# A planned encoder kernel: x is normalised before its split, projections are evacuated straight from PSUM, the pooling matrix goes into the input weights, and the list schedule gets other costs

## The chip, the cores and the metric

The kernel runs on one core of one Trainium2 chip. The metric is the device time of one launch in microseconds (us); lower is better. Engines are named PE (matmul; PEld is its weight load), DVE (vector), ACT (scalar), POOL (GpSimd) and SP (the queue that issues the DMAs here).

## The reference

An encoder of 2 layers with shared weights is applied to two sequences (x_prompt and x_sample) of 1024 tokens and 1024 channels each, and ends in an RMSNorm. One layer is, cut to what matters:

```python
hdn = rmsnorm(x, norm_g)                    # x * rsqrt(mean(x*x) + eps) * g
z = hdn @ w_in                              # 1024 x 3072, 12 blocks of 256 columns
a_v, a_g, b_q, b_k, b_v, b_g, c_u, c_g, d_q, d_k, d_v, d_g = split(z, 12)
y_a = pool_mixer(a_v, pool_w, pool_scale) * silu(a_g)      # (window mean - u) @ pool_w[group] * scale
y_b = dilated_attention(rope(b_q), rope(b_k), b_v) * silu(b_g)
y_c = s5_mixer(c_u, ...) * silu(c_g)                       # SSM over time, gelu, GLU
y_d = neighbourhood_attention(d_q, d_k, d_v, rpb) * silu(d_g)
x = x + concat(y_a, y_b, y_c, y_d) @ w_out
```

The window mean works along time and pool_w along channels, so the two can change places.

## The kernel before

**Layout and number format.** x is kept transposed, 128 channels on the partitions and time along the free dimension, as 8 blocks of 128 channels x 1024 tokens, handled in halves h of 512 tokens. Products with w_in and w_out are made in three terms: each operand is split into a rounded high part (`xh`, `whi`, `yh`) and the rest (`xl`, `wlo`, `yl`), and hi*hi, hi*lo and lo*hi are summed in PSUM (`terms`). One half of one 128-column block of w_in is so 8 x 3 = 24 matmuls of 512 columns.

**Iterations.** `run` goes over 4 iterations (s, l): sequence 0 layer 0, sequence 1 layer 0, sequence 0 layer 1, sequence 1 layer 1; they are numbered 0 to 3 here. Each iteration records the steps of `STEPS`: `na` (neighbourhood attention), `dil` (dilated attention), `ssm` and `sout` (the SSM), `pool`, then `x` (`load_x`: the next iteration's x), `out6723` (the half of the output product that needs y blocks 6, 7, 2 and 3), `out` (the other half). `setup0` and `setup1` make the SSM's tables for a layer.

**From x to a projection.** `load_x` fetches 16 pieces of 128 x 512; `split_x` makes the high part on ACT (scaled with the norm's g) and the rest on DVE. ACT squares each piece and POOL adds the squares. `stats` turns these sums into 1/rms per token (8 small matmuls, a Newton iteration on DVE) and spreads it over the partitions as a tile `rstd` (transposes and ACT copies). rstd isn't in xh and xl; it is multiplied in when a projection leaves PSUM. `project` loads and splits a block of w_in, accumulates a half in a bank of the group mm (3 banks) and calls an evacuation: `scaled` is the DVE product with rstd that writes an SBUF tile of the group z (6 tiles) and frees the bank. What follows works from that tile: `gate` (tanh on ACT, one more DVE product), `split_q` and `split_k` (ACT copies, DVE differences), `rotated` (ACT copies that swap partitions, products with sin and cos on POOL, a DVE sum, then split_q or split_k). `values` makes v with tokens on the partitions and takes rstd as a per-partition scalar.

**Pooling.** `pooling` projects u, sums windows on DVE, takes the difference to u, splits the result and pool_w, multiplies them in three terms (2 halves x 3 matmuls), and DVE multiplies by the scale and the gate.

**The order of the work.** Nothing runs when its line is reached. A `Recorder` takes down every operation with its dependencies; `order` then is a list scheduler that gives each engine a fixed order. It plays time forward: an operation takes `cost` nanoseconds, its results are usable after a latency by pair of engines (`LAT`), and a free engine takes the ready operation with the smallest `prio = idx + cls + base`. `cls` is LATE (+10^6) for the matmuls of `product`, so that projections fill the time in which no other matmul is ready, SOON (-10^6) for evacuations and weight loads. `room` gives a tile out only when all threads can still end. `emit` writes the operations in that order; on the chip each engine takes its instructions in that fixed order and waits at semaphores. `record` treats every access to a PSUM tile as one to the whole bank, and orders two accesses only if one of them writes.

All instructions are issued in one helper, so the profile gives every one the same line, L461; tiles tell them apart. The profile's names follow a buffer's first tile: vz and kt stand for the mm banks (and others), ss and rb for the t banks, ss and rstd for the two tiles that hold rstd, zq, zs, zk, kt and wto for tiles of the group z.

## Time and profile before

| | |
|---|---|
| time, median of 3 runs | 2167.78 us (2164.34 to 2167.82) |
| the profiled execution, its own time | 2156.2 us |
| its span, first to last instruction | 2154.4 us |
| mean granted TensorE clock | 0.975 of full speed |
| instructions | 33356 |

The profile is of one execution. Busy time of an engine is the time in which at least one of its instructions was in work; an idle time has a releaser, what the waiting instruction waited for last. "xN" counts instructions.

### The profile page before, as it was taken

How to read it: one execution, taken by the hardware profiler on the slowest of the kernel's cores; microseconds unless marked ns; L12 is line 12 of the kernel's file. 1: busy time of each engine (PE TensorE's matmuls, PEld its weight loads, DVE VectorE, ACT ScalarE, POOL GpSimd, SP SyncE). 2: the span in 40 equal slices, each digit the busy share in tenths (PEclk: the TensorE clock that was granted, in tenths of full speed). 3: DMA queues.
4: the chain of work that ended last, by engine and by line, in shares of the span. 5: the costliest groups of instructions: out<-in, count | busy, mean ns of one | idle time of the engine just before them, and what ended most of it. 6: DMA issues, size and time to landing. Idle time of an engine off the chain costs nothing.

```text
span 2154.4 us, 33356 instructions
## 1 busy us (share of the span) xinstructions
PE 1984.5 (92%) x10980; PEld 1656.8 (77%) x10980; DVE 1572.2 (73%) x3400; ACT 1095.0 (51%) x2486; POOL 573.6 (27%) x464
## 2 busy tenths in 40 slices
PE   7989999889999999889998999888899999998997
PEld 7757778667888888767787788767678878786777
DVE  7998688987246578788688667888734666888835
ACT  4438595134156688225125678823433766861315
POOL 3218231336200202124017142234543001202103
PEclk8999999999999999999999999999999999999999
DMA  4456535638855444646886543454588645346375
GB/s 160 147 167 188 169 95 169 191 106 269 270 168 160 134 145 118 202 134 217 265 250 187 175 151 105 129 180 155 197 283 278 214 144 173 106 139 201 115 243 178
DMA packets 321853, 381.12 MB, mean 177 GB/s; under 512 B 50832, under 2 KB 196752, under 8 KB 321680
## 3 DMA queue, kind: packets, MB, share of 16 engines
q1 hardware_dynamic: 321680, 378.99, 56.4%
q8 instruction: 87, 1.43, 0.3%
q14 instruction: 86, 0.70, 0.1%
HBM read 268.88 MB, written 112.10 MB: 177 GB/s over the span
## 4 chain that ended last, share of the span: by engine, by line
PE 44%; DVE 22%; DMA 14%; ACT 8%; issue 7%; POOL 3%; SPq 3%; DVEq 0%; POOLq 0%; ACTq 0%
PE vz L461 30%; DMA nv<-vd 4%; PE kt L461 4%; PE no L461 4%; DVE X L461 3%; DMA p<-x 3%; PE ss L461 3%; SPq L461 3%; PE rb L461 2%; DVE p L461 2%; DVE zq L461 1%; DVE gate L461 1%; DVE arena L461 1%; DVE H L461 1%; ACT p L461 1%
## 5 line engine op out<-in xcount | busy, mean ns | idle before, releaser
L461 PE MATMUL vz<-xh,whi 128*128 128x512 f32 x1324 | 531.7, 402 | 3.7 <-DVE zq L461 1.8
L461 PE MATMUL vz<-xl,whi 128*128 128x512 f32 x1324 | 531.5, 401 | 1.5 <-DVE xl L461 1.5
L461 PE MATMUL vz<-xh,wlo 128*128 128x512 f32 x1324 | 530.8, 401 | 0.8 <-POOL wlo L461 0.8
L461 POOL TENSOR_TENSOR wlo<-raw,whi 128x512 fp32r<-128x512 f32 x128 | 179.8, 1406 | 590.7 <-ACT whi L461 437.8
L461 ACT ACTIVATE whi<-raw 128x512 fp32r<-128x512 f32 x248 | 155.6, 627 | 340.5 <-DMA raw<-in_w_in 120.8
L461 PEld LDWEIGHTS vz<-xh,whi 128*128 128x128 f32 x1324 | 251.7, 190 | 49.9 <-issue 2.9
L461 PEld LDWEIGHTS vz<-xh,wlo 128*128 128x128 f32 x1324 | 251.8, 190 | 44.6 <-issue 2.1
L461 PEld LDWEIGHTS vz<-xl,whi 128*128 128x128 f32 x1324 | 252.2, 191 | 43.7 <-DVE xl L461 2.0
L461 PE MATMUL vz<-whi,xh 128*128 128x256 f32 x464 | 135.2, 292 | 15.1 <-ACT xh L461 8.6
L461 ACT ACTIVATE p<-p,st 128x256 f32<-128x256 f32 x256 | 128.3, 503 | 30.6 <-DVE st L461 29.3
L461 DVE TENSOR_TENSOR p<-vz,p 128x512 f32<-128x512 f32 x86 | 58.4, 687 | 112.8 <-DMA p<-x 96.8
L461 PE MATMUL vz<-whi,xl 128*128 128x256 f32 x464 | 134.2, 289 | 0.1
L461 PE MATMUL vz<-wlo,xh 128*128 128x256 f32 x464 | 133.8, 289 | 0.1
L461 PE MATMUL vz<-yh,whi 128*128 128x512 f32 x300 | 121.5, 405 | 9.6 <-DVE p L461 5.2
L461 PE MATMUL vz<-yl,whi 128*128 128x512 f32 x300 | 120.0, 400 | 0.0
L461 PE MATMUL vz<-yh,wlo 128*128 128x512 f32 x300 | 119.5, 400 | 0.0
L461 PEld LDWEIGHTS vz<-whi,xh 128*128 128x128 f32 x464 | 91.3, 197 | 16.9 <-ACT xh L461 8.6
L461 ACT ACTIVATE p<-p,nmx 128x384 f32<-128x384 f32 x128 | 78.2, 612 | 43.1 <-DVE nmx L461 42.1
L461 DVE TENSOR_TENSOR D<-ss,D 128x128 fp32r<-128x128 f32 (+2 forms) x195 | 85.5, 461 | 9.8 <-ACT D L461 8.2
L461 PEld LDWEIGHTS vz<-whi,xl 128*128 128x128 f32 x464 | 91.3, 197 | 1.0 <-issue 0.4
L461 PEld LDWEIGHTS vz<-wlo,xh 128*128 128x128 f32 x464 | 91.2, 197 | 0.8 <-issue 0.4
L461 PE MATMUL no<-D,bv 128*128 128x256 f32 x512 | 88.7, 293 | 3.1 <-DVE D L461 1.5
(489 smaller groups left out, 4616.1 us busy)
## 6 DMA issues: line engine op xcount, KB each, us to landing
raw<-in_w_in SPq DMA_DIRECT2D x192, 256.0 KB
low<-wlo SPq DMA_DIRECT2D x128, 256.0 KB
wlo<-low SPq DMA_DIRECT2D x120, 256.0 KB
x<-p SPq DMA_DIRECT2D x112, 256.0 KB
p<-x SPq DMA_DIRECT2D x88, 256.0 KB
nbias<-in_na_bias SPq DMA_DIRECT2D x48, 384.0 KB
nv<-vd SPq DMA_DIRECT2D x256, 64.0 KB
raw<-in_w_out SPq DMA_DIRECT2D x128, 128.0 KB
```

The costliest lines, as they stand in the source:

```text
L461: getattr(engines[op.eng], op.method)(*[real(a) for a in op.args], **{k: real(v) for k, v in op.kw.items()})
```

## The change

Five things are changed together.

1. `load_x` multiplies a piece by g and rstd on DVE (in place) before it is split, in the iterations 1 to 3. rstd must be known then: the sums of squares are taken where the output product writes the new x (`layer_out`, ACT squares, POOL adds), and for the second sequence's first layer in a new step `sq` (`sum_squares`), of the lowest priority, in iteration 0. `stats` is cut in two: `stats` gives r by token, `spread` makes the rstd tile. Iteration 0 keeps the old way (`self.rstd` isn't None).
2. Evacuations read PSUM: `scaled` returns the bank itself when there is no rstd, and ACT copies or applies tanh, and DVE multiplies, out of the bank. The product with cos moves from POOL to DVE. Evacuations and the split of y run as SOON.
3. pool_w is multiplied into the a_v columns of w_in on the chip (`pool_weights`, steps `poolw0` and `poolw1`, plain fp32 matmuls, result kept in DRAM); the product in `pooling` goes.
4. `cost` has new constants.
5. Factors 0.5 and 0.125 move to other operations.

```diff
-            if op.method == "transpose":
-                return 107 * n / 128
+            if m == "transpose":
+                return 108 * n / 128
             f32r = op.reads[0].dtype == F32R
-            return n / 2.4 + 1 if f32r and n >= 256 else max(n, 128) / 0.6 + 1
+            half = 0.7 if out.dims[0][1] == 64 else 1
+            return n / 2.4 + 13 if f32r and n >= 256 else half * (max(n, 128) / 0.6 + 9)
         if op.eng == "DVE":
-            m = op.method
+
+            wide = sum(v.tile.space == "SB" and v.dims[1:] != [[1, 1]] for v in op.reads) > 1
+            port = 150 if wide and n >= 256 else 0
             if m == "reciprocal":
-                return 68 + 6.5 * n / 0.96
+                return 145 + 6.1 * n
+            if m == "tensor_tensor_scan":
+                return 350 + 2.1 * n
             if not ps and m in ("tensor_copy", "tensor_scalar", "tensor_scalar_mul", "memset"):
-                return 66 + n * 0.525
-            return 68 + n * 1.042 + (8 if m == "tensor_tensor_reduce" else 0) + (61 if isinstance(op.kw.get("scalar"), View) else 0)
+                return 145 + n * 0.53
+            return 145 + n * 1.055 + port + (85 if m == "tensor_tensor_reduce" else 0) + (60 if isinstance(op.kw.get("scalar"), View) else 0)
         if op.eng == "ACT":
-            return (52 if ps else 93) + n * 0.833 + (93 if "accum_out" in op.kw else 0) + (94 if len(op.reads) > 1 else 0)
+            return (180 if ps else 205) + n * 0.833 + (187 if "accum_out" in op.kw else 0) + (88 if len(op.reads) > 1 else 0)
         if op.eng == "POOL":
-            if op.method == "memset":
-                return 40 + n * 0.5
+            if m == "memset":
+                return 90 + n * 0.84
             spread = any(s == 0 and c > 1 for v in op.reads for s, c in v.dims[1:])
-            return 148 + n * (1.67 if spread else 2.1)
+            return 190 + n * (1.8 if spread else 2.4)
...
-        src = self.T[name][l, mt]
+        src = self.T[name][l, mt] if (name, l, mt) not in self.made else self.made[name, l, mt]
...
+    def sum_squares(self, src):
 
         nc = self.nc
         ss = nc.tile([128, S], F32, "rs", "ss")
+        lead = [self.mains[-1]] * 2
+        for h in range(2):
+            sl = slice(512 * h, 512 * h + 512)
+            for k in range(8):
+                sq = self.z("xsq")
+                nc.sync.dma_start(out=sq, in_=src[k, h], after=lead[-2])
+                if k == 0:
+                    lead.append(nc.scalar.activation(ss[:, sl], sq, AF.Square))
+                else:
+                    nc.scalar.activation(sq, sq, AF.Square)
+                    lead.append(nc.gpsimd.tensor_tensor(out=ss[:, sl], in0=ss[:, sl], in1=sq, op=ALU.add))
+        return self.stats([[ss[:, :512]], [ss[:, 512:]]])
+
+    def load_x(self, src, l, r):
+
+        nc = self.nc
+        rstd = self.spread(r)
+        self.rstd = self.rcol = None
         lead = [self.mains[-1]] * 3
         for h in range(2):
             sl = slice(512 * h, 512 * h + 512)
             for k in range(8):
                 raw = self.z("xraw")
                 nc.sync.dma_start(out=raw, in_=src[k, h], after=lead[-3])
-                lead.append(self.split_x(k, sl, raw, l)[0])
-                self.add_square(ss[:, sl], raw, k == 0)
-        self.rstd = self.stats([[ss[:, :512]], [ss[:, 512:]]])
-        self.rcol = self.cols
+                nc.vector.scalar_tensor_tensor(out=raw, in0=raw, scalar=self.norm_g[:, l, k : k + 1], in1=rstd[:, sl], op0=ALU.mult, op1=ALU.mult)
+                lead.append(nc.scalar.activation(self.xh[k][:, sl], raw, AF.Copy))
+                nc.vector.tensor_tensor(out=self.xl[k][:, sl], in0=raw, in1=f32(self.xh[k])[:, sl], op=ALU.subtract)
...
-    def scaled(self, dst, ps, sl, scale=None, shape=lambda a: a):
-
-        nc = self.nc
-        nc.cls = SOON
-        a, b = shape(ps), shape(self.rstd[:, sl])
-        if scale is None:
-            nc.vector.tensor_tensor(out=dst, in0=a, in1=b, op=ALU.mult)
-        else:
-            nc.vector.scalar_tensor_tensor(out=dst, in0=a, scalar=scale, in1=b, op0=ALU.mult, op1=ALU.mult)
-        nc.cls = 0
-
-    def evac_to(self, dst, scale=None):
-        return lambda ps, sl, h: self.scaled(dst(h), ps, sl, scale)
-
-    def gate(self, l, mt, f=0.5):
+    def scaled(self, ps, sl):
+
+        if self.rstd is None:
+            return ps
+        z = self.z("zq")
+        self.nc.vector.tensor_tensor(out=z, in0=ps, in1=self.rstd[:, sl], op=ALU.mult)
+        return z
+
+    def evac_to(self, dst, shape=lambda a: a):
+        def ev(ps, sl, h):
+            self.nc.cls = SOON
+            self.nc.scalar.activation(dst(h), shape(self.scaled(ps, sl)), AF.Copy)
+            self.nc.cls = 0
+        return ev
+
+    def gate(self, l, mt):
 
         nc = self.nc
         g = self.slot([128, S], "gate")
 
         def ev(ps, sl, h):
-            z, th = self.z("zg"), self.z("th")
-            self.scaled(z, ps, sl, f)
-            nc.scalar.activation(th, z, AF.Tanh, scale=0.5 / f)
+            nc.cls = SOON
+            z, th = self.scaled(ps, sl), self.z("th")
+            nc.scalar.activation(th, z, AF.Tanh, scale=0.5)
             nc.vector.scalar_tensor_tensor(out=g[:, sl], in0=th, scalar=1.0, in1=z, op0=ALU.add, op1=ALU.mult)
+            nc.cls = 0
...
-                r = self.rcol[n]
-                nc.scalar.activation(vt[:, i, :, 0], ps, AF.Copy, scale=r)
-                nc.vector.scalar_tensor_tensor(out=vt[:, i, :, 1], in0=ps, scalar=r, in1=f32(vt)[:, i, :, 0], op0=ALU.mult, op1=ALU.subtract)
+                if self.rcol is None:
+                    nc.scalar.activation(vt[:, i, :, 0], ps, AF.Copy)
+                    nc.vector.tensor_tensor(out=vt[:, i, :, 1], in0=ps, in1=f32(vt)[:, i, :, 0], op=ALU.subtract)
...
+            op = self.nc.scalar.activation(at(K[h][d]), z[d], AF.Copy, scale=scale)
+            self.nc.scalar.activation(at(K[h][e]), z[d], AF.Copy, scale=scale)
+            if scale == 1.0:
+                self.nc.vector.tensor_tensor(out=at(kl[h][d]), in0=z[d], in1=at(f32(K[h])[d]), op=ALU.subtract)
+            else:
+                self.nc.vector.scalar_tensor_tensor(out=at(kl[h][d]), in0=z[d], scalar=scale, in1=at(f32(K[h])[d]), op0=ALU.mult, op1=ALU.subtract)
...
-                z = self.z("zq")
-                self.scaled(z.rearrange("p (w r c) -> p r w c", w=4, r=8), ps, sl, None, lambda a: a.rearrange("p (r w c) -> p r w c", r=8, w=4))
-                self.split_q(Q, z.rearrange("p (w x) -> p w x", w=4), lambda t: t.rearrange("p (w g x) -> p g w x", w=4, g=2)[:, h])
+                nc.cls = SOON
+                z = self.scaled(ps, sl).rearrange("p (r w c) -> p w r c", r=8, w=4)
+                self.split_q(Q, z, lambda t: t.rearrange("p (w g r c) -> p g w r c", w=4, g=2, r=8)[:, h])
+                nc.cls = 0
 
             def fk(ps, sl, h):
-                z = self.z("zk")
-                self.scaled(z, ps, sl, 0.125)
-                self.split_k(K, kl, z, lambda t: t[:, sl], h == 0)
+                nc.cls = SOON
+                self.split_k(K, kl, self.scaled(ps, sl), lambda t: t[:, sl], h == 0, 0.125)
...
+            y = self.scaled(ps, sl).rearrange("p (j c) -> p c j", c=4)
             z, zs = self.z("zr"), self.z("zs")
-            self.scaled(by4(z), ps, sl, scale, lambda a: a.rearrange("p (j c) -> p c j", c=4))
             for i in range(4):
                 d, e = 32 * i, 32 * (i ^ 1)
-                nc.scalar.activation(zs[d : d + 32], z[e : e + 32], AF.Copy)
+                nc.scalar.activation(by4(zs)[d : d + 32], y[e : e + 32], AF.Copy, scale=scale)
+            if scale == 1.0:
+                nc.vector.tensor_tensor(out=by4(z), in0=y, in1=by4(cos[:, sl]), op=ALU.mult)
+            else:
+                nc.vector.scalar_tensor_tensor(out=by4(z), in0=y, scalar=scale, in1=by4(cos[:, sl]), op0=ALU.mult, op1=ALU.mult)
+            nc.cls = 0
             nc.gpsimd.tensor_tensor(out=zs, in0=zs, in1=sin[:, sl], op=ALU.mult)
-            nc.gpsimd.tensor_tensor(out=z, in0=z, in1=cos[:, sl], op=ALU.mult)
...
+    def pool_weights(self, l):
+
+        nc = self.nc
+        for m in range(2):
+            made = self.own([128, 8, 128], "wav", F32, "DRAM")
+            wt, pw = self.slot([128, S], "wavt"), self.z("pool_w")[:, :128]
+            nc.sync.dma_start(out=wt, in_=self.T["w_av"][l, m])
+            nc.sync.dma_start(out=pw, in_=self.T["pool_w"][:, l, m])
+            for i in range(2):
+                ps, t = self.bank("t", "wav"), self.z("wav")
+                for k in range(4):
+                    nc.tensor.matmul(ps[:, 128 * k : 128 * k + 128], wt[:, 512 * i + 128 * k : 512 * i + 128 * k + 128], pw, start=True, stop=True)
+                nc.scalar.activation(t, ps, AF.Copy)
+                nc.sync.dma_start(out=made[:, 4 * i : 4 * i + 4], in_=t.rearrange("p (k x) -> p k x", k=4))
+            self.made["w_in", l, MT_AV + m] = made
...
-            pw = self.z("pool_w")[:, :128]
-            nc.sync.dma_start(out=pw, in_=self.T["pool_w"][:, l, m], after=self.mains[-1])
-            if POOLR:
-                pr = self.slot([128, 2, 128], "pwr", F32R)
-                nc.scalar.activation(pr[:, 0], pw, AF.Copy)
-                nc.gpsimd.tensor_tensor(out=pr[:, 1], in0=pw, in1=f32(pr)[:, 0], op=ALU.subtract)
-                wh, wl = self.halves_of(w, "pw")
-            for h in range(2):
-                ps = self.bank("mm", "pool")
-                sl = slice(512 * h, 512 * h + 512)
-                if POOLR:
-                    self.terms(ps, [pr[:, 0]], [pr[:, 1]], [wh[:, sl]], [wl[:, sl]])
-                else:
-                    nc.tensor.matmul(ps, pw, w[:, sl], start=True, stop=True)
-                nc.vector.scalar_tensor_tensor(out=gt[:, sl], in0=ps, scalar=self.pool_s[:, l, m : m + 1], in1=gt[:, sl], op0=ALU.mult, op1=ALU.mult)
+            nc.vector.scalar_tensor_tensor(out=gt, in0=w, scalar=self.pool_s[:, l, m : m + 1], in1=gt, op0=ALU.mult, op1=ALU.mult)
...
-            def f(ps, sl, h, u=u):
-                out = u[:, :, 64 * h : 64 * h + 64].rearrange("p j m -> p m j")
-                self.scaled(out, ps, sl, None, lambda a: a.rearrange("p (m j) -> p m j", j=8))
-
-            self.project(l, MT_CU + m, f, u)
+            tokens = lambda a: a.rearrange("p (m j) -> p j m", j=8)
+            self.project(l, MT_CU + m, self.evac_to(lambda h: u[:, :, 64 * h : 64 * h + 64], tokens), u)
...
+        nc.cls = SOON
         for k in keys:
             nc.scalar.activation(yh[k], self.y[k], AF.Copy, after=self.lead(YLEAD), reserve=[yh[k], yl[k]] if RES else [yh[j] for j in keys] + [yl[j] for j in keys])
             nc.vector.tensor_tensor(out=yl[k], in0=self.y[k], in1=f32(yh[k]), op=ALU.subtract)
+        nc.cls = 0
...
-            if final:
+            if last:
                 self.add_square(ss[:, sl], t, k == 0)
             nc.sync.dma_start(out=self.x[s][k, sl.start // 512], in_=t)
 
         self.output(l, keys, old, write)
+        if last:
+            self.r[s] = self.stats([[ss[:, :512]], [ss[:, 512:]]])
...
-        ("setup0", "na", "dil", "ssm", "sout", "pool", "x", "out6723", "out"),
-        ("na", "dil", "ssm", "sout", "pool", "x", "out6723", "setup1", "out"),
+        ("setup0", "na", "sq", "poolw0", "dil", "ssm", "sout", "pool", "x", "out6723", "out"),
+        ("na", "dil", "ssm", "sout", "pool", "x", "out6723", "setup1", "poolw1", "out"),
...
+    r["w_av"] = w[:, :, 128 * MT_AV : 128 * MT_AV + 256].transpose(0, 2, 1).reshape(depth, 2, 128, 1024)
```

## Rows read from the trace of the kernel before

**Rows 1.** The page, part 1: busy us, share of the span, instructions.

```profile
PE 1984.5 (92%) x10980; PEld 1656.8 (77%) x10980; DVE 1572.2 (73%) x3400; ACT 1095.0 (51%) x2486; POOL 573.6 (27%) x464
```

**Rows 2.** Busy time by engine in iterations 0 and 1: stretch, its length, engines.

```profile
core 0: us, PE busy (x) PEld busy (x) DVE busy (x) ACT busy (x) POOL busy (x), PEclk, DMA share, GB/s
0.00:602.00 602.00, 540.84 (x2993) 451.86 (x2994) 459.02 (x1015) 290.26 (x649) 209.66 (x170) 0.96 0.56 175
602.00:1085.00 483.00, 452.98 (x2441) 376.02 (x2441) 355.04 (x838) 257.64 (x592) 76.69 (x61) 0.99 0.56 174
```

**Rows 3.** Busy time, same columns: SSM and pooling stretches, and output stretches.

```profile
1404.00:1458.00 54.00, 45.87 (x280) 36.80 (x280) 48.70 (x63) 8.90 (x16) 18.05 (x18) 0.97 0.60 181
1458.00:1512.00 54.00, 48.47 (x234) 37.30 (x233) 45.89 (x57) 17.46 (x24) 23.50 (x18) 0.97 0.48 156
...
1566.00:1645.00 79.00, 77.29 (x393) 65.35 (x394) 25.64 (x51) 23.26 (x36) 33.94 (x28) 0.98 0.83 270
...
1944.00:1998.00 54.00, 45.10 (x281) 37.58 (x281) 46.04 (x57) 8.39 (x13) 15.49 (x16) 0.91 0.61 194
...
2052.00:2106.00 54.00, 51.98 (x226) 41.72 (x224) 15.26 (x20) 12.02 (x17) 0.00 (x0) 1.00 0.86 271
```

**Rows 4.** Timeline of PE, iteration 3's SSM: start, length, operation, idle before.

```profile
1940.48 0.39 PE L461 MATMUL vz<-xh,wlo 128*128 128x512 f32 x1
1943.78 0.46 PE L461 MATMUL rb<-H,Cm 128*128 128x128 f32 x2 [2.92 <-issue]
1944.00 0.48 PE L461 MATMUL vz<-xh,whi 128*128 128x512 f32 x1
```

**Rows 5.** Timeline of DVE in the same stretch.

```profile
1930.97 0.68 DVE L461 TENSOR_TENSOR X<-vz,R 128x512 f32<-128x512 f32 x1
1931.57 0.68 DVE L461 TENSOR_TENSOR X<-X,zs 128x512 f32<-128x512 f32 x1
...
1932.77 1.08 DVE L461 TENSOR_TENSOR cu<-vz,ss 128x512 f32<-128x512 f32 x1
1933.68 1.20 DVE L461 TENSOR_TENSOR_SCAN X<-zq,X 128x512 f32<-128x512 f32 x1
...
1941.12 0.67 DVE L461 TENSOR_TENSOR H<-X,zs 64x508 f32<-64x508 f32 x1
```

**Rows 6.** Groups of DVE, 1890 to 2052: count, busy us, mean ns, idle before.

```profile
L461 DVE TENSOR_TENSOR cu<-vz,ss 128x512 f32<-128x512 f32 x4 | 4.4, 1091 | 0.1
...
L461 DVE TENSOR_TENSOR pu<-vz,ss 128x512 f32<-128x512 f32 x4 | 2.7, 683 | 3.4 <-PE vz L461 3.4
...
L461 DVE SCALAR_TENSOR_TENSOR zq<-vz,ss 128x512 f32<-128x512 f32 x4 | 2.7, 682 | 0.4 <-POOL pwr L461 0.4
```

**Rows 7.** ACT's operations out of bank vz: ns min/median/max, first and last start.

```profile
L461 ACT ACTIVATE ct<-vz,c_glu_b x16: 687/687/690, 463.3 to 2022.2; 128x512 f32<-128x512 f32 x16
```

**Rows 8.** Groups over the whole span: count, busy us, mean ns, idle before.

```profile
L461 DVE TENSOR_TENSOR X<-X,R 128x512 f32<-128x512 f32 x32 | 40.4, 1276 | 5.5 <-POOL zq L461 2.4 <-POOL wto L461 1.8 <-POOL kt L461 1.1
...
L461 DVE TENSOR_TENSOR bacc<-bacc,bf 128x1024 f32<-128x1024 f32 x16 | 21.8, 1367 | 9.0 <-DMA bf<-f 8.8
...
L461 DVE SCALAR_TENSOR_TENSOR xl<-xraw,c_norm_g,xh 128x512 fp32r<-128x512 f32 x16 | 19.2, 1230 | 7.7 <-ACT xh L461 7.7
...
L461 PE MATMUL vz<-pwh,pwr 128*128 128x512 f32 x32 | 12.9, 419 | 5.9 <-DVE zq L461 4.0 <-ACT pwh L461 1.8
...
L461 DVE TENSOR_TENSOR X<-vz,R 128x512 f32<-128x512 f32 x16 | 10.9, 684 | 9.6 <-PE vz L461 9.5
```

**Rows 9.** The chain that ended last, output stretch of iteration 0: start, us, what.

```profile
535.42 8.16 PE vz L461 x36
```

**Rows 10.** Timeline of ACT, iteration 1's neighbourhood attention.

```profile
638.63 0.63 ACT L461 ACTIVATE whi<-raw 128x512 fp32r<-128x512 f32 x1
639.36 0.28 ACT L461 ACTIVATE D<-ss 128x128 fp32r<-128x128 f32 x1
```

**Rows 11.** Timeline of DVE, same stretch.

```profile
638.92 0.41 DVE L461 TENSOR_TENSOR D<-ss,D 128x256 fp32r<-128x256 f32 x1
```

**Rows 12.** Timeline, a K half of iteration 1.

```profile
624.83 2.60 ACT L461 ACTIVATE K<-zs 64x512 fp32r<-64x512 f32 x4 [2.26 <-DVE zs L461]
```

More of the change, by code (lines that the diff above doesn't have):

```diff
@@ L206, in cost @@
     def cost(self, op):
-        out = op.writes[0]
+        out, m = op.writes[0], op.method
         n = 1
@@ L633, in first_x @@
         self.ident = self.load("ident", [128, 128])
-        self.rstd = self.stats(squares)
-        self.rcol = self.cols
+        r = self.stats(squares)
+        self.rstd, self.rcol = self.spread(r), [r[:, i : i + 1] for i in range(8)]
     def split_x(self, k, sl, raw, l):
@@ L660, in add_square @@
         if first:
-            nc.scalar.activation(ss, x, AF.Square)
-        else:
-            sq = self.z("sq")[:, : ss.shape[1]]
-            nc.scalar.activation(sq, x, AF.Square)
-            nc.gpsimd.tensor_tensor(out=ss, in0=ss, in1=sq, op=ALU.add)
+            return nc.scalar.activation(ss, x, AF.Square)
+        sq = self.z("sq")[:, : ss.shape[1]]
+        op = nc.scalar.activation(sq, x, AF.Square)
+        nc.gpsimd.tensor_tensor(out=ss, in0=ss, in1=sq, op=ALU.add)
+        return op
     def stats(self, squares, width=512):
@@ L686, in stats, with spread @@
             nc.vector.scalar_tensor_tensor(out=r, in0=a, scalar=1.5, in1=r, op0=ALU.add, op1=ALU.mult)
+        nc.cls = 0
+        return r
+    def spread(self, r, width=512):
+        nc = self.nc
+        nc.cls = SOON
+        m, n = width // 128, r.shape[1]
         rstd = nc.tile([128, S], F32, "rs", "rstd")
-        self.cols = [r[:, i : i + 1] for i in range(n)]
-        for j in range(len(squares)):
+        for j in range(n // m):
             pb = self.bank(SB, "rb")
@@ L1117, in combine @@
         V.reciprocal(m, da)
-        tt(e1, e1, m, ALU.mult)
-        tt(e2, e2, m, ALU.mult)
+        for e in (e1, e2):
+            V.scalar_tensor_tensor(out=e, in0=e, scalar=0.5, in1=m, op0=ALU.mult, op1=ALU.mult)
         d1, d2 = self.dram([2, S], "f1"), self.dram([2, S], "f2")
@@ L1582, in output @@
         held = [None] * 8
+        nc.cls = SOON
         for k in keys:
@@ L1608, in layer_out @@
         final = last and l == self.depth - 1
-        ss = nc.tile([128, S], F32, "rs", "ss") if final else None
+        ss = nc.tile([128, S], F32, "rs", "ss") if last else None
         if final and s == self.nseq - 1:
@@ L1674, in run @@
         self.ssm_tab = [None] * self.depth
-        self.mains, self.rcol, self.lows = [], [], {}
+        self.r = [None] * self.nseq
+        self.mains, self.rcol, self.lows, self.made = [], [], {}, {}
         iters = [(s, l) for l in range(self.depth) for s in range(self.nseq)]
```

39 lines of the change are left out of this document (25 added, 14 removed).

## The prediction

> **What bounds the kernel now.** I read the page's busy times first, then the busy times by iteration and by stretch, then what DVE does in the stretches where PE idles, then single places of the timeline.
>
> PE is busy 1984.5 of 2154.4 us [rows 1], so at most 169.9 us of the span is PE idle, and no change of this kind can win more than that plus what it takes off PE's work. Four iterations (two sequences, two layers) run one after the other; PE idles 61.2 us in the first, called 0 here, and 30.0 in the next [rows 2]. Within an iteration there are two kinds of stretch [rows 3]. Where the output projection runs, PE is full and DVE is nearly free: 25.64 of 79 us busy in 1566 to 1645, 15.26 of 54 in 2052 to 2106. Before that, in the SSM and pooling part, DVE is the fullest engine beside PE (48.70, 45.89, 46.04 of 54 us), ACT is almost idle (8.90 and 8.39 in two of the rows) and PE idles 8.1, 5.5 and 8.9 us per row. The reader should see that one engine is short of time exactly where another has nothing to do.
>
> What PE's idle time looks like there: at 1940.48 it starts the last matmul of a run of projection matmuls, then starts nothing until 1943.78, where the product with H comes, and right behind it stands the next projection matmul, which needed nothing new [rows 4]. DVE writes H from 1941.12 on [rows 5]. PE is served in the order that the list schedule wrote down, and the schedule believed H would be there earlier. So part of the idle time is DVE's work, and part is an order built on wrong durations.
>
> **The change part by part.** The sum is made against the profiled execution, 2156.2 us, of which 2154.4 is span. The median of the runs is 2167.78, 11.6 us more; I add that at the end.
>
> *Multiplications by rstd leave the evacuations (iterations 1 to 3).* An iteration evacuates 40 half projections, each with one DVE product with rstd. Eight of them (rotary) get a product with cos in its place, so 32 go. DVE products of 512 elements start 0.60 us apart (1930.97, 1931.57) though each lasts 0.68 [rows 5]; removing one frees 0.60. In the busy stretch 1890 to 2052 there are 16 such products: 4 cu, 4 pu, and 8 of gates, of which the first row shows 4 [rows 6]. The cu ones last 1.09; the one at 1932.77 holds DVE until 1933.68, 0.91. Sum 12 x 0.60 + 4 x 0.91 = 10.8 us per iteration. Between none of it (PE busy with other work anyway) and all of it reaches the end; I take two thirds, since DVE is the fuller engine there and PE idles 8.9 us in the middle third of that stretch alone [rows 3]: 3 x 7.2 = 21.6, so **-21** (0 to -32). The gates' last products and the q and k differences also lose an SBUF operand, which where POOL runs beside is worth up to 1.276 - 0.684 [rows 8]; that is left to the range. ACT takes over cu and pu, 8 copies. No row has a strided PSUM copy on ACT: the nearest are ACT's tanh out of PSUM, 0.69, and the strided DVE evacuation, 1.09 [rows 6, 7]. That is 5.5 to 8.7 us per iteration, hidden in ACT's 45 idle us of 54; without that cover it would cost just that.
>
> *The pooling product goes into the weights.* 48 matmuls of 512 columns leave PE (the row of one of its kinds has 32 of them, [rows 8]); 36 such matmuls take 8.16 us [rows 9], 0.227 each: -10.9. New are 32 plain fp32 products of 128 columns, each two records; two records of such a size take 0.22 us, from 1943.78 to 1944.00 [rows 4], so 32 x 0.22 = +7.0. Together **-4** (-11 to +3, where an fp32 product with its wait costs double). POOL's split of w and ACT's copy go too; both stand behind the first 192 output matmuls (192 x 0.227 = 44 us), which need no pooled y, so 0; uncovered, their going would be a further gain.
>
> *The new load of x.* A block now takes a DVE product, an ACT copy and a DVE difference, in that order, where it was an ACT copy and one DVE operation. That adds one DVE operation on two SBUF operands per block: 0.68 us (a product with only one SBUF operand) to 1.23 (the mean of the old operation) [rows 8], 16 blocks, 11 to 20 us of DVE per iteration. The work that hides it is the output projection, 384 matmuls x 0.227 = 87 us in which DVE has the room shown above; x is due only when the next values product starts behind them. **0**; 11 to 20 us per iteration if it falls among the pooling work in front. The squares and rstd move an iteration ahead, where POOL and ACT have room; also 0.
>
> *Iteration 0* keeps its rstd products, gains 8 DVE products with cos (POOL's until now; 0.60 to 1.23 each, [rows 5, 8], 5 to 10 us), 8 ACT copies, and the 16 squares of the second sequence with their loads, planned last of all. PE idles 61 us there, which can take it: **+4** (0 to 12).
>
> *Evacuations now keep a PSUM bank shared by ACT and DVE.* Before, DVE emptied it once. Now a K half has four ACT copies and two DVE differences on one bank, a rotary half four ACT copies and one DVE product. At 638.92 DVE reads bank ss until 639.33; ACT, done with whi at 639.26, starts its next copy out of ss at 639.36 [rows 10, 11]. So readers of one bank look as if they took turns, and the planner, which lets two readers run together, doesn't know. Today's four K copies from SBUF run in one piece of 2.60 us [rows 12]; a turn of DVE's adds about 0.7. Twelve such halves per iteration: 8.4 us of ACT waiting, which is busy 257.6 of 483 us [rows 2]. I let a quarter through: 3 x 8.4 / 4 = **+6** (0 to 25). The Trainium skill (PSUM — Partial Sum Buffer, PSUM bank collisions) says that two engines may not touch one bank in the same quadrant at once and that readers count too; the row agrees, and read strictly, with all of that waiting on the path, the 25 would stand in the sum in place of 6 and the end would be 19 us later, 2147.
>
> *The schedule's durations.* Old costs for 512 elements: DVE 0.60, PE 0.214; new 0.685 (0.835 with two SBUF operands) and 0.226. PE measures 0.227 [rows 9]: the new value is right. DVE on PSUM and SBUF lasts 0.684, on two SBUF operands 1.276, and a 1024 product 1.367 where old said 1.135 and new says 1.375 [rows 8]: the new values are nearer where POOL runs beside. But in an unbroken run DVE starts every 0.60, which the old value had exactly. So truer lateness of results, exaggerated occupancy. Nothing in the trace shows the new order; its effect lies between winning half of the about 149 us of idle time left (-70) and rival D below (+53). I take a sixth of the 149, **-25**, since the stall at 1940.48 is of the kind that a later H in the plan cures.
>
> Everything else (the factors 0.5 and 0.125 that move, the values without rcol) swaps one instruction for one of like size: 0.
>
> Sum: 2156.2 - 21 - 4 + 0 + 4 + 6 - 25 = 2116; plus 11.6, **2128 us**, 1.8% faster. PE's own work hardly falls, so nearly all of it must appear as PE idle time going from 170 to about 134 us.
>
> **Rivals.**
>
> *B, the new order is worth more.* With -70 for the schedule: 2071, so 2083. For it: idle time with ready matmuls behind it, as shown. Against: 61 us of the idle time are iteration 0's, which the edits load further.
>
> *C, hidden anyway.* DVE's relief is filled with other waits, the costs hide as well, and only PE's work counts: 2152, so 2164, no change that counts. For it: where PE is full DVE doesn't matter. Against: the SSM rows of [rows 3].
>
> *D, the order gets worse; slower.* The plan books DVE 14% too long in unbroken runs (0.685 against 0.60), so it sets more projection matmuls between attention steps, and those then lack in the SSM stretch, where they are what PE does while DVE works. Price: 14% of the 94.3 us that PE is busy in 1404 to 1512 [rows 3], 13 us, in four iterations 53: 2194, so 2206. It turns the result to slower from 15 us on, a bit over a quarter of that. The Trainium skill (Perfetto Trace Analysis, Optimizing Scalar/DVE Operations) states that a profiled Scalar or DVE duration holds a write acknowledgement that overlaps with the next instruction, so busy time is shorter. The 0.60 against 0.68 agrees. By that rule alone the measured durations are wrong costs for occupancy, and the time would be D's.
>
> *F, the load of x shows.* If DVE's 11 to 20 us per load come before the output matmuls have room for them, 33 to 59 us are added in three loads, 46 in the middle: 2174. For it: three dependent steps per block. Against: 87 us of cover.
>
> **How the numbers follow.** Forecast 0.50, B 0.15, C 0.13, D 0.14, F 0.08. The forecast's own range is 2095 to 2155 (its bounds, not all at once). From B to short of D: 2075 to 2185, which leaves out most of D and a little of B. A measurement here tells about 0.2%, 4 us. Faster: the forecast and B whole, and some of C and F, 0.70; same 0.09, the bulk of C; slower: D, most of F, some of C, 0.21.
>
> **What would show it.** Right: DVE busy down by some 10 us in each SSM stretch (over the span little changes: -66 for 96 products of 0.69, +33 to 59 for three loads, +5 to 10 in iteration 0), PE idle down in the rows that answer to the SSM rows of [rows 3], PE busy about the same; a product with H that no longer waits 3 us with projections behind it. C: DVE falls and PE's idle time doesn't. D: PE idle less in the attention part and more in the SSM part. F: idle time at the values product of iterations 1 to 3. The bank turns: ACT waiting for DVE at K and zs. The number fails above all if the new order moves the idle time by tens of us either way, which no row of before can show.

## The result, and the profile after

The changed kernel takes **2101.14 us** (median of 4 runs, 2094.47 to 2104.17); the kernel before, on the same chip, 2166.06 (2162.55 to 2167.82). The ratio is 0.9702, with a 95% interval of 0.9676 to 0.9728: 3% faster, inside the range, 27 us below the forecast.

The page, part 1, of the changed kernel, beside [rows 1]:

```profile
PE 1960.8 (93%) x10996; PEld 1642.7 (78%) x10996; DVE 1531.7 (73%) x3353; ACT 1124.0 (54%) x2510; POOL 514.7 (25%) x416
```

PE idles 2100.1 - 1960.8 = 139.3 us, where it was 169.9; the forecast said about 134. But PE's busy time fell too, by 23.7, where the forecast had 4. The next two fences are busy times by engine in the four iterations, of the kernel before and of the changed one. A stretch ends where the next iteration's first values matmul starts. The columns are those of [rows 2].

```profile
0.00:578.80 578.80, 517.64 (x2802) 428.85 (x2803) 455.57 (x1008) 284.58 (x638) 207.77 (x169) 0.96 0.56 175
578.80:1084.80 506.00, 475.98 (x2631) 398.83 (x2630) 358.30 (x843) 263.12 (x603) 78.58 (x63) 0.99 0.56 173
1084.80:1629.20 544.40, 504.27 (x2766) 417.14 (x2764) 406.06 (x804) 276.17 (x624) 208.80 (x162) 0.97 0.59 183
1629.20:2154.40 525.20, 486.63 (x2786) 412.01 (x2785) 352.31 (x746) 271.18 (x623) 78.48 (x71) 0.98 0.56 176
```

```profile
0.00:604.40 604.40, 526.35 (x2821) 432.27 (x2822) 474.41 (x1031) 317.90 (x660) 214.07 (x165) 0.93 0.56 177
604.40:1099.50 495.10, 472.56 (x2658) 398.68 (x2658) 330.53 (x773) 264.97 (x610) 57.26 (x53) 0.99 0.58 183
1099.50:1602.20 502.70, 484.51 (x2746) 404.47 (x2746) 408.40 (x838) 269.13 (x615) 184.86 (x139) 1.00 0.62 197
1602.20:2100.10 497.90, 477.37 (x2773) 407.28 (x2773) 318.35 (x713) 272.01 (x628) 58.47 (x60) 0.99 0.59 186
```

Length less PE's busy time is PE's idle time: it goes from 61.2, 30.0, 40.1 and 38.6 us to 78.1, 22.5, 18.2 and 20.5. Iteration 0 became 25.6 us **longer**, the other three 10.9, 41.7 and 27.3 shorter. In iteration 2 the granted clock rose from 0.97 to 1.00, and PE's busy time fell by 20 us with almost as many matmuls: fewer waits, faster matmuls.

Now one SSM, that of iteration 1: from 15 us ahead of its first product with H to its last. First all engines, then only the matmuls that read xl, one in three of the projections. Before:

```profile
875.00:948.00 73.00, 60.30 (x368) 50.62 (x365) 63.46 (x86) 11.04 (x19) 19.07 (x20) 0.93 0.60 192
...
875.00:948.00 73.00, 21.63 (x53) 0.93 0.60 192
```

After:

```profile
912.00:986.00 74.00, 71.28 (x433) 60.01 (x431) 64.87 (x89) 20.68 (x32) 19.81 (x19) 1.00 0.69 216
...
912.00:986.00 74.00, 31.06 (x78) 1.00 0.69 216
```

DVE is as full as it was (63.46 of 73 us, 64.87 of 74), but PE fits 78 such matmuls beside it instead of 53, and idles 2.7 us instead of 12.7. What [rows 4] showed, a wait ahead of the product with H with projections behind it, is gone from iterations 1 to 3. PE's timeline of the changed kernel:

```profile
980.80 0.39 PE L467 MATMUL vz<-xl,whi 128*128 128x512 f32 x1
981.03 0.38 PE L467 MATMUL rb<-H,Cm 128*128 128x128 f32 x2
981.17 0.48 PE L467 MATMUL vz<-xh,wlo 128*128 128x512 f32 x1
```

In the same stretches of iterations 2 and 3 PE idles 4.4 and 2.1 us, where it was 13.3 and 11.8; in iteration 0 nothing was won there (14.3, then 15.1). Waits of 2 us and more ahead of the product with H were eleven, 36.4 us in all, and are now one, 4.02 us in iteration 0.

What iteration 0 lost, in the timelines of PE, DVE, ACT and POOL:

```profile
346.94 0.39 PE L467 MATMUL vz<-xh,wlo 128*128 128x512 f32 x1
361.90 0.80 PE L467 MATMUL vz<-xh,whi 128*128 128x512 f32 x1 [14.57 <-DVE wto L467]
...
354.64 0.21 DVE L467 TENSOR_TENSOR wto<-th 32x64 f32<-32x64 f32 x1 [14.82 <-POOL E L467]
...
355.19 0.40 ACT L467 ACTIVATE wto<-wto 32x64 f32<-32x64 f32 x2 [15.58 <-DVE wto L467]
...
353.35 1.26 POOL L467 TENSOR_TENSOR E<-E,wto 128x512 f32<-128x512 f32 x1
```

PE waits 14.57 us for a z tile's product (wto) of DVE. DVE itself had stood for 14.82 us on POOL's E, a part of the SSM's setup, which runs beside iteration 0's attention, and ACT for 15.58 behind DVE: three engines were ordered behind one background step. When POOL was done, four strided ACT copies (th<-wto, 356.70 to 361.12) still had to read the z tile before DVE could write it again. Another new wait comes from the folded weights: PE waits for a small load of pool_w at the end of iteration 1.

```profile
1063.12 2.05 PE L467 MATMUL rb<-th,wavt 128*128 128x128 f32 x8 [7.84 <-DMA th<-in_pool_w]
```

### The profile page after: what moved, and what is told of

Its sections match the earlier page's. It is cut to its first block, busy times and chain, and to the rows that moved or that the text cites. A ratio compares the mean times of both kernels' runs of the same rounds, so it can differ in the third digit from the quotient of the medians.

```text
span 2100.1 us, 33288 instructions
## 1 busy us (share of the span) xinstructions
PE 1960.8 (93%) x10996; PEld 1642.7 (78%) x10996; DVE 1531.7 (73%) x3353; ACT 1124.0 (54%) x2510; POOL 514.7 (25%) x416
## 4 chain that ended last, share of the span: by engine, by line
PE 47%; DMA 14%; DVE 9%; issue 3%; SPq 2%; ACT 2%; POOL 0%; DVEq 0%; ACTq 0%; POOLq 0%
PE vz L467 34%; PE kt L467 4%; DMA nv<-vd 4%; PE no L467 4%; DMA p<-x 3%; PE rb L467 3%; PE ss L467 3%; SPq L467 2%; DMA x<-p 1%; DVE p L467 1%; DMA raw<-in_w_out 1%; DVE X L467 1%; DVE H L467 1%; DVE arena L467 1%; DVE wto L467 1%
## 5 line engine op out<-in xcount | busy, mean ns | idle before, releaser
L467 PE MATMUL vz<-xh,whi 128*128 128x512 f32 x1316 | 525.2, 399 | 16.7 <-DVE wto L467 14.6
L467 PE MATMUL vz<-xl,whi 128*128 128x512 f32 x1316 | 525.4, 399 | 0.3 <-DVE xl L467 0.3
L467 POOL TENSOR_TENSOR wlo<-raw,whi 128x512 fp32r<-128x512 f32 x128 | 193.0, 1510 | 479.5 <-ACT whi L467 387.5
L467 PE MATMUL vz<-whi,xl 128*128 128x256 f32 x480 | 139.9, 292 | 0.5 <-DVE xl L467 0.3
L467 PE MATMUL vz<-wlo,xh 128*128 128x256 f32 x480 | 138.9, 291 | 0.0
L467 ACT ACTIVATE p<-p,st 128x256 f32<-128x256 f32 x256 | 128.1, 503 | 13.3 <-DVE st L467 11.9
L467 PE MATMUL vz<-yh,whi 128*128 128x512 f32 x288 | 115.7, 402 | 14.8 <-DVE p L467 10.6
L467 PE MATMUL vz<-yh,wlo 128*128 128x512 f32 x288 | 113.4, 395 | 0.6 <-DMA wlo<-low 0.6
L467 PE MATMUL vz<-yl,whi 128*128 128x512 f32 x288 | 113.4, 394 | 0.0
L467 DVE TENSOR_TENSOR D<-rb,D 128x256 fp32r<-128x256 f32 (+2 forms) x212 | 91.9, 454 | 19.7 <-ACT D L467 18.1
L467 ACT ACTIVATE D<-rb 128x256 fp32r<-128x256 f32 (+2 forms) x212 | 80.5, 412 | 31.1 <-PE rb L467 28.8
```

Of the source, the lines that this page charges most:

```text
L467: getattr(engines[op.eng], op.method)(*[real(a) for a in op.args], **{k: real(v) for k, v in op.kw.items()})
```

## The experiments

| | kernel | us | ratio to before (95%) |
|---|---|---|---|
| 1 | before, new durations | 2246.31 | 1.0384 (1.0339 to 1.0429) |
| 2 | after, old durations | 2182.46 | 1.0075 (1.0044 to 1.0106) |
| 3 | after, shorter fixed parts for DVE and ACT | 2225.2 | 1.0278 (1.0235 to 1.0321) |
| 4 | after, old pooling product | 2149.14 | 0.9926 (0.9901 to 0.9951) |
| 5 | 1 with 8 z tiles | 2210.1 | 1.019 (1.0158 to 1.0222) |
| 6 | after, PSUM copied out by DVE first | 2122.43 | 0.979 (0.9764 to 0.9816) |
| 7 | after, all durations times 1.01 | 2117.26 | 0.9771 (0.975 to 0.9792) |
| 8 | before, all durations times 1.01 | 2168.02 | 1.0008 (0.9987 to 1.0029) |
| 9 | 1 with SOON as in the change | 2142.43 | 0.9871 (0.9829 to 0.9912) |
| 10 | after, yh and yl not SOON | 2207.03 | 1.0169 (1.0127 to 1.0211) |
| 11 | after with 8 z tiles | 2094.39 | 0.9666 (0.9632 to 0.9701) |
| 12 | before with SOON as in the change | 2158.72 | 0.9956 (0.9935 to 0.9977) |

Each ratio is to runs of the kernel before beside it (medians 2166.79 to 2168.06 us). Differences in us below are against 2166.06 for before and 2101.14 for the changed kernel, if nothing else is said.

**1. The durations alone.** The kernel before with the function `cost` of the change:

```diff
-            return 68 + n * 1.042 + ...
+            return 145 + n * 1.055 + port + ...
```

> The kernel before with the new cost function alone; every operation is as before, only the order differs. Theory: the truer durations are the larger part of the 65 us (consumers of DVE results are put later in PE's order, so PE idles less): 2110 to 2130 us. Rival: the edits are the larger part, the new order is worth little by itself: 2145 to 2166 us. If measured durations are wrong as costs of occupancy (rival D of the prediction), above 2170 us.

2246.31 us, 80 slower than before, where only rival D's outcome had a loss. Timelines of PE, DVE and ACT in iteration 1's SSM:

```profile
987.68 0.61 PE L467 MATMUL rb<-H,Cm 128*128 128x128 f32 x4
999.80 1.35 PE L467 MATMUL ss<-H,Cm 128*128 128x128 f32 x4 [11.51 <-issue]
...
993.95 0.63 ACT L467 ACTIVATE zq<-zq 128x512 f32<-128x512 f32 x1 [4.96 <-DVE X L467]
996.53 0.68 DVE L467 SCALAR_TENSOR_TENSOR gate<-zq,zq 128x512 f32<-128x512 f32 x1
997.24 0.63 ACT L467 ACTIVATE zq<-th 128x512 f32<-128x512 f32 x1 [2.67 <-DVE gate L467]
999.62 0.68 DVE L467 TENSOR_TENSOR H<-X,wto 64x508 f32<-64x508 f32 x1
1000.33 0.69 DVE L467 SCALAR_TENSOR_TENSOR gate<-zq,th 128x512 f32<-128x512 f32 x1
```

PE waits 11.51 us ahead of the product with H, and no projection stands ahead of it. All four SSMs have such a wait (457, 988, 1543 and 2079 us). The gates' tanh (zq<-zq, zq<-th) and product (gate) stand among the SSM's X and H work; until they are done they hold z tiles. The projections' matmuls in this stretch:

```profile
937.00:1004.00 67.00, 8.60 (x22) 0.75 0.41 124
1004.00:1064.00 60.00, 15.61 (x40) 1.00 0.57 181
```

22 in the SSM, where before had 53, and 40 in the 60 us behind it, where before had 46. Of the iteration's 320 such matmuls 258 came ahead of the SSM, where before had 221. So 37 were drawn forward, and those that were left were not ready in the order while PE waited. The granted clock fell to a mean of 0.75.

**2. The edits without the durations.** The changed kernel with the old `cost`.

> The changed kernel with the old cost function; all edits, the old durations. Theory: the edits alone give what the prediction's terms for them sum to, -15 us, so 2145 to 2160 us. Rival: the edits are the larger part, 2100 to 2125 us. If edits and costs only work together, 2166 us or more here and in the run with the costs alone.

2182.46 us, 16 slower than before. So neither the durations (+80) nor the edits, SOON among them, (+16) help without the other, and together they win 65.

**3. What a duration should say.** The changed kernel with the fixed parts of DVE and ACT as in the old costs, the other new terms kept:

```diff
-            return 145 + n * 1.055 + port + ...
+            return 68 + n * 1.055 + port + ...
```

> The changed kernel, but DVE's and ACT's fixed parts are those of the old cost function (start to start in an unbroken run, 0.60 us for 512 elements), while the new terms for two SBUF operands, for PE, POOL and scans stay. Theory: what helps is that results come later in the plan, so taking these 80 to 130 ns per instruction away loses part of the gain: 2115 to 2145 us. Rival D: exaggerated occupancy costs time, so this is faster than the changed kernel: 2070 to 2095 us. If neither matters: 2096 to 2108 us.

2225.2 us, 124 slower than the changed kernel, far more than the theory's loss and the contrary of rival D's outcome. The last 77 ns of a DVE step, which the next step overlaps, and the last 112 to 128 ns of an ACT step are no ballast here. Half of the loss is iteration 0, 669 us long. PE's timeline there has the reduction of the second sequence's squares, planned far ahead of POOL's sums:

```profile
293.41 1.86 PE L467 MATMUL ss<-ones,ss 128*128 128x1 f32 x8 [22.82 <-POOL ss L467]
```

**4. The pooling product as it was.** The changed kernel without the folded weights, with the product behind the pooling as before.

> The changed kernel with the pooling product where it was before (and no weights made on the chip). Theory: 4 us of PE work more and little else: 2102 to 2110 us. Rival: in the changed kernel PE waits 7.8 us for the load of the pooling matrix near 1055 us and 3.9 us near 164 us, both for the products that make these weights, so without them the kernel is faster: 2085 to 2098 us.

2149.14 us, more than either expectation: undoing the fold costs 48, where its work on PE is worth 4. In the profiled execution iterations 0, 2 and 3 are 19.0, 24.4 and 8.4 us longer, iteration 1 only 0.4, so this is not a fixed price of each product. PE's timeline behind the SSM of iteration 0 now has a wait for the glu weights' load:

```profile
517.83 2.90 PE L467 MATMUL vz<-cy,gw 128*128 128x512 f32 x3 [9.58 <-DMA gw<-in_glu_w]
```

The changed kernel waits 0.2 us for that load. Why it comes late was not tried.

**5. More z tiles.** Experiment 1 with `SIZES` z = 8 instead of 6 and A = 20 instead of 21.

> The kernel before with the new cost function (2246 us) and two more tiles in the group z (8 in place of 6), paid for with one tile of the group A (20 in place of 21). Theory Z: with the new durations the SSM's temporaries keep the z tiles longer in the plan, evacuations that need a z tile can't empty their bank, and so no projection is there to fill PE's four waits of 11.7 us for H; with more z tiles the waits fill up and the time is 2120 to 2180 us. Rival: the projections have been drawn forward and used up, as rival D of the prediction says; z tiles don't matter, 2230 to 2260 us.

2210.1 us, 36 less than experiment 1 and between the two expectations. The projections' matmuls in iteration 1's SSM and in the 60 us behind it:

```profile
914.00:985.00 71.00, 27.32 (x69) 1.00 0.58 182
985.00:1045.00 60.00, 2.34 (x6) 0.67 0.33 100
```

69 instead of 22: held z tiles were what kept the projections out. But now only 6 are left for the time behind the SSM, and there the clock falls to 0.67: the wait has moved.

**6. What reading PSUM itself is worth.** The changed kernel, but from iteration 1 on DVE copies each half projection out of PSUM first, and the rest reads the copy. The cosine product is POOL's again, the rotary copies read in order and without SOON, and DVE writes cu and pu; these three are undone in iteration 0 too. The edit's main lines:

```diff
         if self.rstd is None:
-            return ps
+            self.nc.vector.tensor_copy(z, ps)
+            return z
```

> The changed kernel with one edit undone: DVE copies each half projection from its bank to SBUF first (in place of the product with rstd, and the cos product on POOL), as before; x still comes normalised, new costs. Theory Z: the evacuations need z tiles again and DVE gets its 32 operations per iteration back, the waits for H with nothing behind them return, 2180 to 2250 us. Rival: reading PSUM matters only by DVE's time, at most 32 us in three iterations, so 2110 to 2135 us.

2122.43 us, 21 more than the changed kernel, as the rival had it. Of theory Z's waits for H two came back, of 3.32 and 6.85 us. In the profiled execution iterations 1 to 3 are 37 us longer and iteration 0 is 17 shorter.

**7 and 8. How much a reshuffle moves.** `op.cost = 1.01 * self.cost(op)` in the changed kernel and in the one before.

> The changed kernel with every planned duration 1% longer: no edit, no other relation of the costs. It shows how far the time moves by a mere reshuffle. If the gain is a property of the changed kernel: 2090 to 2115 us. If the order is a lottery of some per cent: anywhere from 2070 to 2170 us.

> The kernel before with every planned duration 1% longer, the same reshuffle. If its time is a property of the kernel: 2155 to 2180 us. If the order is a lottery: anywhere from 2120 to 2230 us; a kernel before that is one of the better draws would move up.

+16 and 0, the first 2 us past what was expected of a property of the kernel. An order that is no better in intent can move the changed kernel by 16 us, so single differences of that size carry no verdict on a mechanism.

**9. The priority, with the durations.** The diff also puts more work under SOON, the list schedule's early class: all steps of an evacuation instead of its first, and the yh and yl copies. (Of a rotation these are the copies, and in the change the cosine product too.) Experiment 1 plus that alone, without the cosine product:

```diff
+            self.nc.cls = SOON
             evac(ps, sl, h)
+            self.nc.cls = 0
...
+        nc.cls = SOON
         for k in keys:
             nc.scalar.activation(yh[k], ...)
             nc.vector.tensor_tensor(out=yl[k], ...)
+        nc.cls = 0
```

> The kernel before with the new durations, as in the first experiment (2246.31 us), and with the priority SOON over every step of an evacuation (tanh, product, head splits, the copies and the cosine product of a rotation) and over the yh/yl copies, as the change has it; no other edit. Theory S: the new durations alone lose because the later steps of an evacuation wait in the plan behind the SSM's own DVE and ACT work and hold their z tiles, so that no bank is emptied and no projection is ready when the product with H waits. Then the 11.5 us waits ahead of ss<-H,Cm are filled with projections (each below 4 us) and the time falls by 80 us or more, to 2110 to 2165 us, which is near the sixth experiment (2122.43). Rival N: it is the rstd products and their z tiles as such, which this kernel still has; then the waits of 11 us stay in at least three of four SSMs and the time stays at 2215 to 2260 us. Between 2165 and 2215 both have a part.

2142.43 us, 104 less than experiment 1, as theory S had it. The projections' matmuls in iteration 1's SSM:

```profile
890.00:973.00 83.00, 31.29 (x78) 0.98 0.60 190
```

78, as in the changed kernel; no wait ahead of the product with H reaches 2 us. But no projection is left for the 60 us behind this SSM, where PE is busy 37.12 us at a granted clock of 0.74, and iteration 1 gains only 4 of the 104. There this kernel has the wait of experiment 4, 11.73 us for the glu weights:

```profile
988.95 2.07 PE L467 MATMUL vz<-cy,gw 128*128 128x512 f32 x2 [11.73 <-DMA gw<-in_glu_w]
```

Which of the two parts of SOON did it was not run apart. In experiment 1 PE never waits 1 us for yh or yl, so the evacuations are the likelier part.

**10. The priority undone in the changed kernel,** for the yh and yl copies alone.

> The changed kernel with one thing undone: the yh/yl copies at the head of each output projection have the ordinary priority again instead of SOON (two lines). Theory S1: those copies free the slots of the y tiles and let the output projections start; without SOON they come late, and the stretches of the SSM and the output of iterations 1 to 3 wait again: 2150 to 2230 us, with new PE waits of over 5 us that end on yh or yl or ahead of ss<-H,Cm. Rival N1: the splits are few (16 instructions in an iteration) and have room: 2085 to 2118 us, what a reshuffle of this kernel's order moves (its durations times 1.01 moved it by 16 us).

2207.03 us, 106 more than the changed kernel, for two lines: S1. PE's and DVE's timelines at the output of iteration 1:

```profile
1046.10 0.40 PE L467 MATMUL vz<-yh,whi 128*128 128x512 f32 x1
1067.78 0.80 PE L467 MATMUL vz<-yl,whi 128*128 128x512 f32 x1 [21.28 <-DVE yl L467]
...
1047.54 0.74 DVE L467 SCALAR_TENSOR_TENSOR zq<-zq,c_norm_g,ss 128x512 f32<-128x512 f32 x1
...
1065.89 0.70 DVE L467 TENSOR_TENSOR xl<-wto,xh 128x512 fp32r<-128x512 f32 x1
1066.50 1.23 DVE L467 TENSOR_TENSOR yl<-gate,yh 128x1024 fp32r<-128x1024 f32 x1
```

From 1047.54 to 1066.5 DVE does nothing but the next x (zq, th, wto scaled, then xl), 19 us of it; yl comes behind, and PE waits 21.28 us for it. Iterations 0 and 2 have the same wait, 16 and 21 us; the three together are 58.5 of the 106.

**11. More z tiles in the changed kernel.**

> The changed kernel with z = 8 tiles instead of 6 and one slot of group A less (20 for 21), to pay for them in SBUF. Theory Z: iteration 0, which grew from 570 to 596 us, waits for z tiles that the SSM's setup holds (the 14.6 us at 346.94); with two more, that wait is below 5 us, iteration 0 takes 570 to 585 us and the kernel 2070 to 2090 us. Rival: z tiles bind no more and one A slot less costs: 2095 to 2130 us, with iteration 0 at 590 us or more. Within 16 us of 2101 alone the time does not decide, since a reshuffle moves as much; the wait and the length of iteration 0 do.

2094.39 us (2092.58 to 2101.26), between the two expectations and within a reshuffle of the changed kernel. Busy times in iteration 0:

```profile
0.00:581.50 581.50, 520.73 (x2821) 430.47 (x2821) 471.45 (x1031) 317.65 (x660) 209.96 (x165) 0.95 0.58 184
```

The long wait is gone and iteration 0 is 22.9 us shorter than the changed kernel's 604.4 (the 596 of the expectation, counted to the boundary used here), so z tiles were its limit; the others take 499.4, 511.8 and 501.2 us, 4.3, 9.1 and 3.3 longer, and give 17 of it back. Whether that is the missing A slot or a reshuffle stays open.

**12. The priority alone.** The kernel before with experiment 9's lines and its own durations.

> The kernel before with its own durations and nothing but the wider priority: SOON over every step of an evacuation and over the yh/yl copies, as in the ninth experiment (2142.43 us, which has the new durations as well). It fills the fourth corner beside before (2168), the durations alone (2246) and both (2142). Theory P: the priority is worth something by itself, because short durations made the plan believe that the later steps of an evacuation were done long before they were; 2135 to 2160 us, so that the new durations add next to nothing to it on this kernel. Rival J: the two only work together, as the durations move H late enough for projections to be wanted and the priority makes them ready; then this kernel stays at 2155 to 2185 us, with waits of 2 us and more ahead of the product with H and projections behind them, as before.

2158.72 us, 0.44% faster (8 us against 2166.79 beside it). In the overlap of both expectations; PE's timeline speaks for J, since the waits ahead of the product with H are still there, the longest of iteration 1 here:

```profile
929.41 0.77 PE L461 MATMUL ss<-H,Cm 128*128 128x128 f32 x2 [3.41 <-issue]
```

## Why the forecast came out 27 us high

**The sum and the base.** 2116 was to be the profiled time; that is 2101.9, 14 less. The other 12 come from the base: I added 11.6 us, because the profiled execution of before ran below its median. The changed kernel's median is 0.8 below its profiled time. That the sum came so near is in part luck. Two errors of opposite sign stand between experiment 9, which has the durations and SOON, and the changed kernel, which has the other edits as well: in the profiled executions iteration 0 is 24.6 us longer (forecast 4), and the other three are 67.6 shorter, where the forecast had 19 for all of them (21 and 4, less 6).

**Where PE idles, and why: right.** Stretches in which DVE is full and PE waits for H with ready projections behind it; these filled up in iterations 1 to 3 (12.7 to 2.7 us in iteration 1), though not by a later H alone, with which the waits grew (1). The sign I expected on DVE was wrong: its busy time doesn't fall in the SSM stretch, more work goes through beside it. DVE is relieved elsewhere (358.30 to 330.53 us in iteration 1, 352.31 to 318.35 in iteration 3); in iteration 2, which won most, its busy time didn't fall (406.06 to 408.40).

**Schedule's durations, -25: the failed step.** I took them for one term, added to the edits'. They aren't additive: +80 on the kernel before (1), -81 in the changed kernel (2182.46 to 2101.14, 2). And "everything else: 0" passed over the one part of the diff that joins them, SOON over whole evacuations and over yh and yl. With the new durations it is worth 104 (9 against 1), and with a part of it undone the kernel loses 106 (10); with the old ones 8 (12). On the kernel before, durations and SOON together give 24 (2166.06 to 2142.43), nearly the 25 forecast for the durations alone; that is luck too, as the durations alone lose 80. Longer durations keep more steps waiting in the plan at a time, so which goes first decides: steps that free a z tile or feed the output, or X and H. That reading is the one that 5, 9 and 10 fit together; the plan's own queue was not recorded.

**Rival D** had the sign of experiment 1 and half of its mechanism. Projections were drawn forward as it said (258 instead of 221), but in the changed kernel, which is faster, 240 come ahead of the SSM too; the loss came with the 40 that were left and not ready. And booking less time for DVE and ACT made the changed kernel slower (3), where D wanted the contrary. The trace still agrees with the rule of the Trainium skill (Perfetto Trace Analysis, Optimizing Scalar/DVE Operations): in experiment 10 DVE steps that last 0.69 start 0.60 apart. It didn't decide the time.

**Rstd products, -21: the sign is right, the size open.** The 21 us of 6 are 37 lost in iterations 1 to 3 and 17 won in iteration 0; 6 undoes the turns at a bank and the move of the cosine product as well, and a reshuffle is 16.

**Pooling product, -4: mis-sized.** PE's part is as costed: 64 records came, 48 went (10980 to 10996 matmuls). I gave the rest 0, covered by 44 us of output matmuls. It wasn't covered in that order: putting the product back costs 48 (4), three times a reshuffle, with waits of 8.07 for H and 9.58 for the glu weights at the end of iteration 0's SSM. How much of the 48 is the product and how much the order stays open, as iteration 1 lost nothing.

**The load of x, 0: right, on a condition I had not seen.** The cover holds because yl goes first. Without SOON the load's DVE work, 19 us, stands ahead of yl (10), and rival F's picture is there: its three waits are 58.5 us, F's upper price 59, though the kernel loses 106. The work itself was put too high: over three loads the products and differences take 83.9 us of DVE where the old operations took 58.6, 8.4 more per load and not 11 to 20.

**Iteration 0, +4 (0 to 12): mis-sized,** 25.6. Most of it comes with the edits: iteration 0 takes 579.8 us in experiment 9, which has only the durations and SOON, and 597.1 in 2, which has the edits with the old durations. z tiles held by background work make a wait of 14.57 (11 removes it). And the rotary copies, which I took for ones of like size, became 1.8 times as long on ACT, since they now read with a stride of four elements. Groups of ACT in iteration 0, after, and before:

```profile
L467 ACT ACTIVATE th<-wto 32x512 f32<-32x512 f32 x8 | 8.9, 1110 | 0.8 <-DVE wto L467 0.6 <-POOL ss L467 0.2
```

```profile
L461 ACT ACTIVATE zk<-zq 32x512 f32<-32x512 f32 x8 | 5.0, 630 | 2.1 <-DVE zq L461 1.9
```

32 such copies at 1.11 instead of 0.63 are 15 of the 33 us by which ACT's busy time grew there (284.58 to 317.90).

**Turns at a bank, +6: the wait is there.** ACT between the two pairs of a K half, timeline and group, iterations 1 to 3:

```profile
650.53 1.20 ACT L467 ACTIVATE K<-vz 64x512 fp32r<-64x512 f32 x2 [0.75 <-DVE kl L467]
...
L467 ACT ACTIVATE K<-vz 64x512 fp32r<-64x512 f32 x48 | 28.4, 592 | 19.6 <-PE vz L467 10.1 <-DVE kl L467 9.2
```

ACT waits 0.75 for the DVE difference; 9.2 us over 12 K halves, 0.77 each where I had 0.7. Ahead of the 96 rotary copies it waits another 14.6 us for DVE, so with them 23.8 where the forecast had 25; which of the 14.6 is a bank and which a z tile the groups don't tell. The profile puts these waits down to a semaphore, so they are waits of the program: the second pair of K copies reads the other 64 partitions of the bank than the DVE difference it waits for, and no run shows whether the chip would have needed them to take turns. What reaches the end was not told apart; 6, without these turns, is slower all the same.

## What to carry to other kernels

When a list schedule gets truer durations, its priorities are part of the change: price what frees a scarce buffer and what feeds the fullest engine, and look which of them queue behind long background work. Terms of an order couldn't be added here: run the durations and the edits each alone before either is believed. And a change of 1% in all durations, one more order of the same intent, gives a first size for what is only a reshuffle.

## What the runs showed of the hardware

A wait is paid twice. Behind the 14.57 us the projections' matmuls start 0.43 us apart, later 0.23; the granted clock of the changed kernel:

```profile
361.90:365.00 3.10, 3.10 (x7) 2.48 (x8) 2.21 (x4) 3.02 (x5) 0.56 (x1) 0.50 0.31 84
365.00:368.00 3.00, 3.00 (x10) 2.38 (x9) 1.39 (x3) 1.71 (x3) 0.29 (x1) 0.66 0.99 281
368.00:371.00 3.00, 3.00 (x15) 2.51 (x15) 2.28 (x3) 2.91 (x5) 1.01 (x1) 1.00 0.79 246
```

0.50 is 1.2 GHz, 1.00 is 2.4. A dozen matmuls ran at the lower level, 12 x 0.20 = 2.4 us on top of the wait.

ACT's strided copies take longer out of SBUF (1110 ns, 630 in order, above), but not out of PSUM (589): the same rotary copy of iterations 1 to 3, and the reordered cu, which I had put at 690 to 1090:

```profile
L467 ACT ACTIVATE th<-vz 32x512 f32<-32x512 f32 x32 | 18.8, 589 | 5.8 <-DVE wto L467 4.5 <-DVE th L467 0.8 <-PE vz L467 0.3
...
L467 ACT ACTIVATE cu<-vz 128x512 f32<-128x512 f32 x12 | 7.1, 593 | 3.4 <-PE vz L467 3.2
```
